# Hybrid decoder step on one core: gate rows ahead of sample factors, projections' second halves in another accumulator ring, old x ahead of output weights

## Chip, cores and metric

The kernel runs on one core of one Trainium2 chip. The metric is the device time of one execution in microseconds; lower is better. The kernel before takes 1245.87 us, the median of three runs (1245.64 to 1247.6).

## The reference, cut to what matters

The program computes one inference step of a two-layer decoder trunk, in float32, for a prompt of 512 positions and 8 single-token samples. Both share the weights, so the kernel treats them as 520 columns (T = 520, TP = 512, TS = 8). The width is 1024, the heads are 4 of 256.

```python
def block(x, c, C0, n0, m0, mbuf0, cbuf0, ...):
    mod = jax.nn.silu(c) @ w_ada + b_ada
    shift, scale, gate = jnp.split(mod[:, None, :], 3, axis=-1)
    h = rmsnorm(x, norm_w) * (1.0 + scale) + shift
    xm, zm, ga, gb, zc, gm, gc = jnp.split(h @ w_in, N_SPLITS, axis=-1)
    xm_c, mbuf = causal_dwconv(xm, mbuf0, mconv_w, mconv_b)
    xm_c = jax.nn.silu(xm_c)
    q = jnp.einsum('bthd,hde->bthe', xc_h, w_q)
    k = jnp.einsum('bthd,hde->bthe', xc_h, w_k) * (HEAD_DIM ** -0.5)
    v = jnp.einsum('bthd,hde->bthe', xm_h, w_v)
    g = (qkv @ w_gate + b_gate).astype(jnp.float32)
    i_pre = jnp.swapaxes(g[..., :N_HEADS], 1, 2)
    logf = jnp.swapaxes(jax.nn.log_sigmoid(g[..., N_HEADS:]), 1, 2)
    hm, C, n, m = mlstm_chunkwise(q, k, v, i_pre, logf, C0, n0, m0)
    ...
    u, cbuf = causal_dwconv(ga * jax.nn.sigmoid(gb), cbuf0, cconv_w, cconv_b)
    ...
    merged = jax.nn.sigmoid(gm) * y_m + jax.nn.sigmoid(gc) * y_c
    x = x + gate * (merged @ w_out)
```

The outputs are x after a last norm, and for prompt and samples the new memories C, n, m and the tails of both convolutions.

## The kernel before, in words

Activations lie with channels on the 128 partitions and positions along the free side: 8 tiles of 128 x 520 for a width of 1024. Every float32 product is made of three in a rounded type: a weight tile is cast (`whi`, on ScalarE, L171) and its remainder taken (`wlo`, on GpSimd, four pieces, L174); activations are split likewise (`hh`, `hl`). `dense` (L178) computes one output tile in two halves of 260 columns; each half is an accumulation of 3 matmuls per input tile, 24 for a width of 1024 and 6 for the per-head projections of q, k and v, and ends with an evacuation by ScalarE or VectorE.

Accumulators come from rings of buffers: tag "d" with three for `dense`, tag "m" with three for nearly all else (gate products `pg` and `pf`, the turned gate rows `pst`, sample values `pvt`, value and key transposes `ptok`, score products `pu` and `pds`, the short convolution's accumulator `ac`), tag "cv" with two for the long convolution. A tile waits until the buffer that it is given has been read by its last reader.

Raw weights come by DMA from SyncE's queue (SP), in order, into two buffers; `whi` and `wlo` have three. So a weight load waits for a `wlo`, and a cast waits until TensorE has finished with the weights of three tiles earlier.

A layer runs so: the norm of x with scale and shift gives `hh` and `hl` (`norm_in`, L435); the first product of the convolution branch; for each head `do_xm` (two tiles of xm, the short convolution, then `xcs`, its split), `do_v` and `do_qk` (both through `proj`, L587); gate products and the scans along the positions (L681 to L728); the convolution branch's next products `gab`; the transposes of the gate rows and of the values; a loop over heads with the scores, and with the samples' memories between; then the remaining products, and at the end the output product, which adds the gated result to the old x (`residual`, L323). In layer 0 the old x is loaded tile by tile into `xo`, one of four buffers of tag "t520" (L1113).

In the gate part (L708 to L728), `st` holds rows that are turned (L735) and copied to `stT` (L737), the per-position factors of the scores. `ur` holds rows for the scores in two parts (L714, L715). `lms`, `mn`, `sx` and `xe` (L716 to L728) are the samples' factors, needed by `sample_factors` after head 0's scores; `sxt` is the tile that holds both `st` and `xe`.

The order on each engine is fixed when the program is built: a scheduler plays through the operations with its own estimates and lists each engine's instructions. `tc.issue_after(i)` tells it that a block may not be listed before instruction i. The engines then run their lists in order.

Of the kernel before, what the change touches and what calls it, by code (L numbers as in the profile page):

```python
# [11 lines left out]
F32 = mybir.dt.float32  # L12
F32R = mybir.dt.float32r
I32 = mybir.dt.int32
AF = mybir.ActivationFunctionType
# [8 lines left out]
TP = 512  # L24
# [49 lines left out]
def build(nc, tc, ctx, ap):  # L74
# [103 lines left out]
    def dense(w, xh, xl, nk, evac, halves=(0, 1)):  # L178
        hi, lo = w
        for c in halves:  # L180
            p = pm("pd", "d")
# [230 lines left out]
    for l in range(L):  # L412
# [22 lines left out]
        def norm_in(k):  # L435
# [8 lines left out]
            else:  # L444
                for c in range(2):
                    v.scalar_tensor_tensor(out=t[:, HALF[c]], in0=x[:, k, HALF[c]], scalar=sa[:, k, 0:1], in1=rb[c],
                                           op0=ALU.mult, op1=ALU.mult)
# [13 lines left out]

        u = None
# [124 lines left out]
        def proj(w, src, dst, h, sc):  # L587
            for m in range(2):
                wm = tuple(a[:, m * 256:(m + 1) * 256] for a in w)
                if sc is None:  # L590
                    dense(wm, src[:, 0], src[:, 1], 2, lambda c, p: s.copy(dst[:, 2 * h + m, c], p))
                else:
                    mm = dense(wm, src[:, 0], src[:, 1], 2,
                               lambda c, p: s.activation(dst[:, 2 * h + m, c], p, AF.Copy, scale=sc))
            return mm if sc is not None else None
# [119 lines left out]
        v.tensor_tensor(out=ur[32:48], in0=gF, in1=ur.bitcast(F32)[0:16], op=ALU.subtract)  # L715
        lms = sml.tile([16, TS], F32, name="lms")  # L716
        mn = sml.tile([16, TS], F32, name="mn")
        v.tensor_tensor(out=lms, in0=lf[:, TP:T], in1=rows[0:16, 1:9], op=ALU.add)
        v.tensor_tensor(out=mn, in0=lms, in1=gi[:, TP:T], op=ALU.max)
        nc.sync.dma_start(ap["o_m_s"][l], mn[0:4])  # L720
        sx = sml.tile([16, 3, TS], F32, name="sx")
        v.tensor_tensor(out=sx[:, 0], in0=lms, in1=mn, op=ALU.subtract)
        v.tensor_tensor(out=sx[:, 1], in0=gi[:, TP:T], in1=mn, op=ALU.subtract)
        v.tensor_scalar(out=sx[:, 2], in0=mn, scalar1=-1.0, scalar2=None, op0=ALU.mult)
        s.activation(sx, sx, AF.Exp)
        for hh_ in range(4):
            v.tensor_scalar(out=xe[0:4, :, hh_, S0:32], in0=sx[0:4], scalar1=ident[0:4, hh_:hh_ + 1],
                            scalar2=None, op0=ALU.mult)  # L728
# [505 lines left out]
```

## Time and profile before

| | |
|---|---|
| Median of three runs | 1245.87 us |
| Profiled execution, its time | 1245.75 us |
| Its span, first to last instruction | 1244.0 us |
| Mean granted TensorE clock | 0.992 |
| TensorE, VectorE, ScalarE, GpSimd busy | 97%, 68%, 44%, 52% |
| Gate part and transposes, layer 0 and 1 | 126 to 155 us, 739 to 767 us |
| Projections, layer 0 and 1 | 58 to 126 us, 666 to 739 us |
| Output product of layer 0, norm of layer 1 | 580 to 626 us, 626 to 651 us |

In the profile PE is TensorE's matmuls, PEld its weight loads, DVE VectorE, ACT ScalarE, POOL GpSimd, and SP the queue that issues DMAs. A row of a timeline starts with the start in us from the span's beginning and the duration in us; then come engine, line, operation, output tile, input tiles, shapes and count, and in brackets the engine's idle time before it with what ended it. A row that begins with a window A:B lists its length, then busy time and count of PE, PEld, DVE, ACT and POOL, then the granted clock, the DMA share and GB/s.

### The profile page before, as it was taken

What the parts mean: (1) busy time and instruction counts of PE and PEld (TensorE: products, weight loads), DVE (VectorE), ACT (ScalarE), POOL (GpSimd) and SP (SyncE); (2) the same over time, 40 slices, a digit from 0 to 9 for tenths busy, and PEclk for the clock granted to TensorE, in tenths of its full rate; (3) what the DMA queues carried; (4) which work ended last, traced back from release to release, by engine and by line L of the source; (5) the groups of instructions that cost most, each with busy time, mean ns of one, the idle gap of its engine ahead of it and who ended that gap; (6) DMA issues with size and microseconds to landing.
All of it is one profiled execution on the core that took longest, in us unless ns stands there. A gap on an engine that the chain in (4) does not pass through costs nothing.

```text
span 1244.0 us, 26981 instructions
## 1 busy us (share of the span) xinstructions
PE 1207.4 (97%) x10856; PEld 1161.5 (93%) x10856; DVE 850.7 (68%) x1719; ACT 550.0 (44%) x991; POOL 648.6 (52%) x869
## 2 busy tenths in 40 slices
PE   6999999999999999999999999999999999999996
PEld 5999898899999999999988988988999999999995
DVE  6874467676998896654258635667789999937424
ACT  4676556543422223532236656556333222335242
POOL 2575444457544444565627553555665544536571
PEclk9999999999999999999999999999999999999998
DMA  9423447742364242243913234575332222224222
GB/s 362 148 89 94 146 149 256 266 173 95 104 219 153 91 148 86 78 170 130 366 67 96 87 109 175 195 263 213 125 103 94 94 88 100 86 85 137 104 86 69
DMA packets 59934, 177.23 MB, mean 142 GB/s; under 512 B 13408, under 2 KB 21664, under 8 KB 55712
## 3 DMA queue, kind: packets, MB, share of 16 engines
q1 hardware_dynamic: 56928, 167.08, 38.8%
q10 hardware_dynamic: 2880, 8.42, 1.8%
q8 instruction: 85, 1.39, 0.5%
q14 instruction: 41, 0.34, 0.1%
HBM read 149.77 MB, written 25.71 MB: 141 GB/s over the span
## 4 chain that ended last, share of the span: by engine, by line
PE 87%; DVE 4%; issue 3%; ACT 3%; DMA 2%; POOL 1%; SPq 0%; DVEq 0%; ACTq 0%; POOLq 0%
PE pd L186 72%; PE pds L889 3%; PE ppv L855 2%; PE pcf L855 2%; DMA wada<-w_ada 1%; PE ada L293 1%; PE ptok L850 1%; ACT whi L171 1%; PE pqc L789 1%; POOL wlo L174 1%; PE pg L688 1%; PE pd L246 1%; DMA raw<-wst 1%; PE pth L946 1%; PE pu L885 0%
## 5 line engine op out<-in xcount | busy, mean ns | idle before, releaser
L174 POOL TENSOR_TENSOR wlo<-raw,whi 128x256 fp32r<-128x256 f32 x680 | 523.8, 803 | 498.9 <-ACT whi L171 490.5
L186 PE MATMUL pd<-hh,whi 128*128 128x260 f32 x1728 | 494.9, 287 | 0.0
L186 PE MATMUL pd<-hl,whi 128*128 128x260 f32 x1728 | 492.2, 285 | 0.0
L186 PE MATMUL pd<-hh,wlo 128*128 128x260 f32 x1728 | 491.8, 285 | 0.0
L171 ACT CAST whi<-raw 128x1024 fp32r<-128x1024 f32 (+1 forms) x174 | 179.4, 1032 | 365.2 <-PE pd L186 329.7
L186 PEld LDWEIGHTS pd<-hh,whi 128*128 128x128 f32 x1728 | 326.8, 189 | 3.6 <-issue 1.8
L186 PEld LDWEIGHTS pd<-hh,wlo 128*128 128x128 f32 x1728 | 326.9, 189 | 1.8 <-issue 1.2
L186 PEld LDWEIGHTS pd<-hl,whi 128*128 128x128 f32 x1728 | 326.5, 189 | 1.8 <-issue 0.6
L535 DVE SCALAR_TENSOR_TENSOR cv<-u,vec,cv 128x509 f32<-128x509 f32 (+6 forms) x448 | 296.8, 729 | 0.0
L804 DVE SCALAR_TENSOR_TENSOR cb<-vb,wsk,cb 128x257 f32<-128x257 f32 x128 | 75.0, 651 | 1.1 <-ACT cb L802 0.4
L186 PE MATMUL pd<-hmh,whi 128*128 128x260 f32 x256 | 72.3, 282 | 0.0
L186 PE MATMUL pd<-hml,whi 128*128 128x260 f32 x256 | 72.3, 282 | 0.0
L186 PE MATMUL pd<-hmh,wlo 128*128 128x260 f32 x256 | 72.3, 282 | 0.0
L186 PE MATMUL pd<-zl,whi 128*128 128x260 f32 x256 | 71.6, 282 | 0.0
L186 PE MATMUL pd<-zh,wlo 128*128 128x260 f32 x256 | 71.6, 282 | 0.0
L186 PE MATMUL pd<-zh,whi 128*128 128x260 f32 x256 | 71.4, 282 | 0.0
L186 PE MATMUL pd<-mh,whi 128*128 128x260 f32 x224 | 63.1, 282 | 0.0
L186 PE MATMUL pd<-mh,wlo 128*128 128x260 f32 x224 | 63.1, 282 | 0.0
L186 PE MATMUL pd<-ml,whi 128*128 128x260 f32 x224 | 63.1, 282 | 0.0
L326 DVE SCALAR_TENSOR_TENSOR xr<-pd,mod,xo 128x260 f32<-128x260 f32 (+1 forms) x32 | 14.8, 482 | 60.7 <-PE pd L186 33.6
L186 PE MATMUL pd<-xcs,whi 128*128 128x260 f32 x256 | 48.5, 289 | 1.0
L186 PEld LDWEIGHTS pd<-hmh,wlo 128*128 128x128 f32 x256 | 48.2, 188 | 0.0
(304 smaller groups left out, 2236.7 us busy)
## 6 DMA issues: line engine op xcount, KB each, us to landing
raw<-wst SPq DMA_DIRECT2D x160, 512.0 KB, 3.7
wada<-w_ada SPq DMA_DIRECT2D x36, 512.0 KB, 9.1
cb<-C SPq DMA_DIRECT2D x16, 1028.0 KB, 7.8
o_C_s<-cb SPq DMA_DIRECT2D x16, 1028.0 KB, 5.7
vb<-vsc SPq DMA_DIRECT2D x16, 514.0 KB, 6.3
wada<-w_ada ACTq DMA_DIRECT2D x12, 512.0 KB, 8.0
raw<-wqkv SPq DMA_DIRECT2D x8, 512.0 KB, 3.6
x<-x SPq DMA_DIRECT2D x4, 520.0 KB
```

The lines of the kernel that those rows point to most:

```text
L171: s.copy(hi, sl)
L174: g.tensor_tensor(out=lo[:, cs], in0=sl[:, cs], in1=hi.bitcast(F32)[:, cs], op=ALU.subtract)
L186: mm = te.matmul(p[:, 0:HT], a[:, ws], b[:, k, HALF[c]], start=(n == 0), stop=(n == 3 * nk - 1))
L246: mm = te.matmul(p[:, 0:HT], a[:, ws], b[:, k, HALF[c]], start=(k == 0 and i == 0), stop=(k == KT - 1 and i == 2))
L293: mm = te.matmul(acc[32 * j:32 * j + 32, 0:128], cT[:, k, :], raw[k // 2][:, k % 2, j * 128:(j + 1) * 128], start=(n == 0), stop=(n == KT ...
L326: v.scalar_tensor_tensor(out=x[:, m, c.start:c.start + n], in0=p[:, 0:n], scalar=mod[:, 16 + m, 0:1], in1=xo[:, c.start:c.start + n], op0= ...
L535: v.scalar_tensor_tensor(out=acc[a][:, sft:TP], in0=u[:, k, 0:TP - sft], scalar=wcol(sft), in1=acc[a][:, sft:TP], op0=ALU.mult, op1=ALU.add)
L688: te.matmul(pgs[n][32 * j:32 * j + 32, 0:HT], vec[:, o:o + 32], (q, kk, vv)[t][:, k, c], start=(r == 0), stop=(r == 5))
L789: te.matmul(p[32 * h:32 * h + 32, 0:V1], zq[:, o:o + 32], cb[:, k, :], start=(j == 0), stop=(j == 1))
L804: v.scalar_tensor_tensor(out=cb[:, 2 * h + j, :], in0=vb[:, h, :], scalar=wsk[:, h, j, b:b + 1], in1=cb[:, 2 * h + j, :], op0=ALU.mult, op ...
L855: te.matmul(p, a, b, start=(first and n == 0), stop=(last and n == 2))
L889: te.matmul(p[:, 0:n], kk[:, 2 * h + j, t0:t0 + 128], q[:, 2 * h + j, t0:TP], start=(j == 0), stop=(j == 1))
```

## The change

Four things change. First, the samples' factors and the second part of `ur` are written as a block that may not be listed ahead of the copy to `stT`. Second, in `proj` the second half of each output tile takes its accumulator from "m" instead of "d". Third, in layer 1, the first operation of `norm_in` goes tile by tile in order. Fourth, both old x tiles of a pair of output tiles are loaded ahead of that pair's weights.

```diff
-    def dense(w, xh, xl, nk, evac, halves=(0, 1)):
+    def dense(w, xh, xl, nk, evac, halves=(0, 1), homes=(("d", 3), ("d", 3))):
         hi, lo = w
         for c in halves:
-            p = pm("pd", "d")
+            p = pm("pd", *homes[c])
...
                 for c in range(2):
-                    v.scalar_tensor_tensor(out=t[:, HALF[c]], in0=x[:, k, HALF[c]], scalar=sa[:, k, 0:1], in1=rb[c],
-                                           op0=ALU.mult, op1=ALU.mult)
+                    with tc.issue_after(norm_in.last.ins) if norm_in.last else nullcontext():
+                        norm_in.last = v.scalar_tensor_tensor(out=t[:, HALF[c]], in0=x[:, k, HALF[c]],
+                                                              scalar=sa[:, k, 0:1], in1=rb[c],
+                                                              op0=ALU.mult, op1=ALU.mult)
...
+        norm_in.last = None
...
-                if sc is None:
-                    dense(wm, src[:, 0], src[:, 1], 2, lambda c, p: s.copy(dst[:, 2 * h + m, c], p))
-                else:
-                    mm = dense(wm, src[:, 0], src[:, 1], 2,
-                               lambda c, p: s.activation(dst[:, 2 * h + m, c], p, AF.Copy, scale=sc))
-            return mm if sc is not None else None
+                mm = dense(wm, src[:, 0], src[:, 1], 2,
+                           lambda c, p: (s.copy(dst[:, 2 * h + m, c], p) if sc is None else
+                                         s.activation(dst[:, 2 * h + m, c], p, AF.Copy, scale=sc)),
+                           homes=(("d", 3), ("m", 3)))
+            return mm
...
-        v.tensor_tensor(out=ur[32:48], in0=gF, in1=ur.bitcast(F32)[0:16], op=ALU.subtract)
-        lms = sml.tile([16, TS], F32, name="lms")
...
+        def sample_gates():
+            lms = sml.tile([16, TS], F32, name="lms")
+            mn = sml.tile([16, TS], F32, name="mn")
+            v.tensor_tensor(out=lms, in0=lf[:, TP:T], in1=rows[0:16, 1:9], op=ALU.add)
+            v.tensor_tensor(out=mn, in0=lms, in1=gi[:, TP:T], op=ALU.max)
+            nc.sync.dma_start(ap["o_m_s"][l], mn[0:4])
+            sx = sml.tile([16, 3, TS], F32, name="sx")
+            v.tensor_tensor(out=sx[:, 0], in0=lms, in1=mn, op=ALU.subtract)
+            v.tensor_tensor(out=sx[:, 1], in0=gi[:, TP:T], in1=mn, op=ALU.subtract)
+            v.tensor_scalar(out=sx[:, 2], in0=mn, scalar1=-1.0, scalar2=None, op0=ALU.mult)
+            s.activation(sx, sx, AF.Exp)
+            for hh_ in range(4):
+                v.tensor_scalar(out=xe[0:4, :, hh_, S0:32], in0=sx[0:4], scalar1=ident[0:4, hh_:hh_ + 1],
+                                scalar2=None, op0=ALU.mult)
...
-        v.tensor_copy(stT, pt.rearrange("p (b r) -> p b r", b=4)[:, :, 0:36])
+        turned = v.tensor_copy(stT, pt.rearrange("p (b r) -> p b r", b=4)[:, :, 0:36])
+        with tc.issue_after(turned.ins):
+            v.tensor_tensor(out=ur[32:48], in0=gF, in1=ur.bitcast(F32)[0:16], op=ALU.subtract)
+            sample_gates()
...
+            xos = [t520("xo") for _ in range(2)]
+            for j in range(2):
+                nc.sync.dma_start(xos[j], x_src[:, m0 + j, :])
             ws = split_w(ap["wst"][l, PR_OUT + m0 // 2], 2)
             for j in range(2):
                 m = m0 + j
-                xo = t520("xo")
-                nc.sync.dma_start(xo, x_src[:, m, :])
-                mm = dense(ws[j], mh, ml, KT, residual(x, xo, mod, m))
+                mm = dense(ws[j], mh, ml, KT, residual(x, xos[j], mod, m))
```

Line numbers of the changed program are 2 to 5 higher than before behind the first edit. In the rows below a line stands first, then the operation, the tile written and the tiles read.

**Place 1, the gate part of layer 0.** VectorE before, up to the copy to `stT` (`us` is a copy for the long convolution of the samples, `upr` its product, made on GpSimd):

```order
L713 TENSOR_TENSOR g_1718<-g_1718 16x512
L722 TENSOR_TENSOR sx<-lms,mn 16x8
L723 TENSOR_TENSOR sx<-g_1718,mn 16x8
L724 TENSOR_SCALAR sx<-mn 16x8
L508 COPY us<-u 128x8
L714 CAST ur<-g_1718 16x512
L727 TENSOR_SCALAR sxt<-sx,ident 4x3x8 x2
L715 TENSOR_TENSOR ur<-g_1718,ur 16x512
L727 TENSOR_SCALAR sxt<-sx,ident 4x3x8 x2
L513 TENSOR_REDUCE u<-upr 128x8
L514 TENSOR_SCALAR u<-u,vec 128x8
L737 COPY stT<-pst 128x144
```

`lms` (L718) and `mn` (L719) stand a few rows further up. VectorE now:

```order
L715 TENSOR_TENSOR g_1718<-g_1718 16x512
L511 COPY us<-u 128x8
L716 CAST ur<-g_1718 16x512
L516 TENSOR_REDUCE u<-upr 128x8
L517 TENSOR_SCALAR u<-u,vec 128x8
L739 COPY stT<-pst 128x144
L741 TENSOR_TENSOR ur<-g_1718,ur 16x512
L720 TENSOR_TENSOR lms<-g_1718,rows 16x8
L755 COPY vtok<-pvt 128x256
L757 COPY qk<-pvt 128x1
L721 TENSOR_TENSOR mn<-lms,g_1718 16x8
L724 TENSOR_TENSOR sx<-lms,mn 16x8
```

The second part of `ur`, `lms`, `mn`, `sx` and the four `sxt` rows moved behind the copy; the `sxt` rows now stand directly ahead of the split of the values, `v1l`. ScalarE at the same place before, from the samples' exponential `sx` to the first score exponential `dd` (`en` is an exponential of the turned rows, `v1h` the values' cast):

```order
L725 ACT_TABLE_LOAD
L725 ACTIVATE sx<-sx 16x24
L553 COPY sg<-pd 128x260
L171 CAST whi<-raw 128x1024
L553 COPY sg<-pd 128x260
L739 ACTIVATE en<-stT 128x16
L579 ACT_TABLE_LOAD
L579 ACTIVATE sg<-sg 128x520
L872 CAST v1h<-ptok 128x2x256 x2
L892 ACT_TABLE_LOAD
L892 ACTIVATE dd<-pu,stT 128x512
```

ScalarE now:

```order
L556 COPY sg<-pd 128x260
L744 ACT_TABLE_LOAD
L744 ACTIVATE en<-stT 128x16
L582 ACT_TABLE_LOAD
L582 ACTIVATE sg<-sg 128x520
L727 ACT_TABLE_LOAD
L727 ACTIVATE sx<-sx 16x24
L877 CAST v1h<-ptok 128x2x256 x2
L897 ACTIVATE dd<-pu,stT 128x512
```

The exponential `sx` moved behind the sigmoid of `sg`, with its table load; the load ahead of `dd` is gone, so the count of loads is the same.

**Place 2, the projections of layer 1.** ScalarE before, at the values of head 0 (`vv`); the buffer numbers tell the halves apart, in the order of the code 8713, 8721, 8729, 8737:

```order
L608 COPY xm_8641<-pd_8644 128x260
L609 CAST xms_8642<-pd_8644 128x260
L171 CAST whi_8818<-raw_8816 128x1024
L608 COPY xm_8641<-pd_8671 128x260
L609 CAST xms_8642<-pd_8671 128x260
L591 COPY vv_8465<-pd_8713 128x260
L616 ACTIVATE ac_8700<-xm_8641,vec_8297 128x512
L591 COPY vv_8465<-pd_8721 128x260
L631 ACTIVATE xc_8459<-acs_8489,vec_8297 128x8 x2
L591 COPY vv_8465<-pd_8729 128x260
```

ScalarE now (8713 and 8729 are first halves, in "d"; 8721 and 8737 second halves, in "m"):

```order
L610 COPY xm_8641<-pd_8644 128x260
L611 CAST xms_8642<-pd_8644 128x260
L171 CAST whi_8818<-raw_8816 128x1024
L610 COPY xm_8641<-pd_8671 128x260
L611 CAST xms_8642<-pd_8671 128x260
L594 COPY vv_8465<-pd_8713 128x260
L618 ACTIVATE ac_8700<-xm_8641,vec_8297 128x512
L594 COPY vv_8465<-pd_8729 128x260
L594 COPY vv_8465<-pd_8721 128x260
```

The cast `whi_8818` stands where it stood, ahead of the two evacuations of 8671. The first half 8729 moved ahead of the second half 8721; TensorE has the same order, and puts all three ahead of the next dense product, 8745, where before all four halves stood ahead of it.

**Place 3, the end of the projections of layer 0.** TensorE before, from the last but one half to the first gate product:

```order
L186 MATMUL pd_1693<-xcs_1638,wlo_1632 128x260
L186 MATMUL pd_1701<-xcs_1638,whi_1631 128x260 x2
L186 MATMUL pd_1701<-xcs_1638,wlo_1632 128x260
L186 MATMUL pd_1701<-xcs_1638,whi_1631 128x260 x2
L186 MATMUL pd_1701<-xcs_1638,wlo_1632 128x260
L688 MATMUL pg_1721<-vv_613,vec_322 32x260 x2
```

TensorE now:

```order
L186 MATMUL pd_1693<-xcs_1638,wlo_1632 128x260
L186 MATMUL pd_1812<-hh_303,whi_1795 128x260
L186 MATMUL pd_1812<-hl_304,whi_1795 128x260
L186 MATMUL pd_1812<-hh_303,wlo_1796 128x260
L186 MATMUL pd_1701<-xcs_1638,whi_1631 128x260 x2
L186 MATMUL pd_1701<-xcs_1638,wlo_1632 128x260
L186 MATMUL pd_1701<-xcs_1638,whi_1631 128x260 x2
L186 MATMUL pd_1701<-xcs_1638,wlo_1632 128x260
L186 MATMUL pd_1812<-hh_303,whi_1795 128x260
L186 MATMUL pd_1812<-hl_304,whi_1795 128x260
L186 MATMUL pd_1812<-hh_303,wlo_1796 128x260
L690 MATMUL pg_1721<-vv_613,vec_322 32x260 x2
```

Six matmuls of the next product, 1812, moved ahead of the gate products; layer 1 has the same. In the whole gate part 117 of them instead of 123 then stand between the second `pf` and `pst`.

Elsewhere: in the norm of layer 1 VectorE does both halves of a tile before the next tile, so the first tile's are the first two of the 8 that stand ahead of the first `hl`, with 2 small ones (`hs`) where 3 stood. TensorE has 36 matmuls of the modulation ahead of the last column sums where it had 48. On SP the two loads of a pair of `xo` stand together, ahead of the weights' loads of the pair after.

More of the change, by code (lines that the diff above doesn't have):

```diff
@@ L714, in build @@
         v.tensor_copy(ur[0:16], gF)
-        v.tensor_tensor(out=ur[32:48], in0=gF, in1=ur.bitcast(F32)[0:16], op=ALU.subtract)
-        lms = sml.tile([16, TS], F32, name="lms")
[L717 to L728, printed above, removed]
+        def sample_gates():
[12 more added lines that the diff above has]
+                                scalar2=None, op0=ALU.mult)
         gab(1, raw=True)
```

## The prediction

> **What bounds the kernel now.** I read the page first, then the chain of waits, then what TensorE itself waits for.
>
> ```profile
> PE 1207.4 (97%) x10856; PEld 1161.5 (93%) x10856; DVE 850.7 (68%) x1719; ACT 550.0 (44%) x991; POOL 648.6 (52%) x869
> PE 87%; DVE 4%; issue 3%; ACT 3%; DMA 2%; POOL 1%; SPq 0%; DVEq 0%; ACTq 0%; POOLq 0%
> 292.06 65.43 PE pd L186 x544
> ```
>
> TensorE (PE) is busy 97% of 1244.0 us. The change removes no matmul, so all it can win is idle TensorE time and time at a lower clock. The third row, a stretch of the chain without a gap, gives the pace: 65.43 / 544 = 0.12 us from one matmul to the next. The waits of TensorE by engine and line say where the idle time is:
>
> ```profile
> PE ptok L850 <- DVE stT L737: 4.6, 2, 2.3
> PE pd L186 <- ACT xms L609: 3.5, 6, 2.7
> PE pd L186 <- ACT kk L594: 1.5, 2, 0.8
> ```
>
> The columns are total us, times, longest. The first row is once per layer: the value transposes (ptok) need an "m" buffer that the turned gate rows (pst) hold until VectorE (DVE) has copied them to stT. The other two lie in the projections. Next the granted clock, in windows (after the idle or busy time of each engine stand PEclk, DMA share and GB/s):
>
> ```profile
> 155.24:158.65 3.41, 3.41 (x17) 3.31 (x16) 1.29 (x2) 3.38 (x5) 0.23 (x1) 0.50 0.97 372
> 670.65:674.06 3.41, 3.40 (x15) 3.40 (x16) 3.41 (x7) 2.99 (x8) 2.88 (x5) 0.50 0.06 9
> 674.06:677.47 3.41, 3.41 (x31) 3.41 (x30) 3.41 (x7) 2.63 (x6) 2.85 (x4) 1.00 0.44 156
> 762.81:766.22 3.41, 1.45 (x38) 1.23 (x36) 3.31 (x14) 1.69 (x4) 2.09 (x3) 1.00 0.35 67
> 11.88:15.29 3.41, 1.86 (x52) 1.05 (x44) 2.88 (x10) 0.00 (x0) 0.00 (x0) 1.00 1.04 401
> PEclk9999999999999999999999999999999999999998
> ```
>
> Behind each wait of 2.3 us or more follows a stretch of 3.41 us at clock 0.50 (the third begins at 766.22, behind the wait in the fourth row). Such a stretch gets 16 matmuls done where a full one gets 31, so it costs 3.41 x (1 - 16/31) = 1.65 us on top of its wait. In the fourth row 1.96 us of 3.41 were idle and the clock fell; in the fifth 1.55 us were idle and it held. I take the limit to lie between the two. The last row, the clock in tenths over 40 slices, shows no other stretch that is long enough to see, but for the tail.
>
> **Part 1, gate rows ahead of sample factors.** VectorE from the end of the scans to the copy:
>
> ```profile
> 147.24 0.62 DVE L718 TENSOR_TENSOR lms<-g,rows 16x8 f32<-16x8 f32 x1
> 147.79 0.67 DVE L711 TENSOR_TENSOR sxt<-g 16x512 f32<-16x512 f32 x1
> 149.38 0.59 DVE L719 TENSOR_TENSOR mn<-lms,g 16x8 f32<-16x8 f32 x1
> 149.89 0.41 DVE L560 TENSOR_TENSOR u<-pd,sg 128x260 f32<-128x260 f32 x1
> 150.83 0.15 DVE L722 TENSOR_TENSOR sx<-lms,mn 16x8 f32<-16x8 f32 x1
> 151.06 0.15 DVE L508 COPY us<-u 128x8 f32<-128x8 f32 x1
> 151.47 0.36 DVE L727 TENSOR_SCALAR sxt<-sx,ident 4x24 f32<-4x24 f32 x2
> 152.90 0.58 DVE L513 TENSOR_REDUCE u<-upr 128x8 f32<-128x248 f32 x1
> 154.02 0.29 DVE L737 COPY stT<-pst 128x144 f32<-128x144 f32 x1
> 157.03 1.29 DVE L873 TENSOR_TENSOR v1l<-ptok,v1h 128x512 fp32r<-128x512 f32 x2 [1.86 <-ACT v1h L872]
> ```
>
> Taken out ahead of the copy, by differences of starts: L718 0.55, L719 0.51, L722 to L724 (150.83 to 151.06) 0.23, and L727, L715, L727 (151.47 to 152.90) 1.43; together 2.72 us. Not all of it comes through: the reduction L513 needs the product that GpSimd makes from the us copy.
>
> ```profile
> 151.29 0.74 POOL L512 TENSOR_TENSOR upr<-us,vec 128x248 f32<-128x248 f32 x1 [1.34 <-DVE us L508]
> ```
>
> The us copy now starts 0.55 + 0.51 + 0.23 = 1.29 earlier, at 149.77; GpSimd is free at 149.95 (151.29 less its idle 1.34), its product ends about 150.75, and L513 starts about 150.8 instead of 150.2. So the copy comes 152.90 - 150.8 = **2.1 us earlier**. Bounds: 2.7, if the product hides, and 1.4, if it takes twice its 0.74.
>
> What is late next? The sample factors' chain, and with it the value copies. ScalarE (ACT) now:
>
> ```profile
> 154.35 0.22 ACT L739 ACTIVATE en<-stT 128x16 f32<-128x16 f32 x1 [1.49 <-DVE stT L737]
> 154.58 1.28 ACT L579 ACT_TABLE_LOAD   x1
> 155.88 0.64 ACT L579 ACTIVATE sg<-sg 128x520 f32<-128x520 f32 x1
> 156.42 1.06 ACT L872 CAST v1h<-ptok 128x512 fp32r<-128x512 f32 x2
> ```
>
> The sample exponential and its table load move between sg and the v1h casts, while the load ahead of L892 goes: as many loads as before, but one is now ahead of v1h. From the end of stT: en 0.22, load 1.28, sg 0.64, load 1.28, sx 0.22 make 3.65; the four L727 (0.15 apart) end at 4.4 and the first v1l (0.65) at 5.1. The score product pds takes the buffer that this v1l frees. TensorE, at full clock, comes there after 4 transposes, pu and 15 + 17 matmuls: 32 x 0.12 and, as an estimate, 0.1 for each of the six small ones = 4.4. So it waits **0.7 us per layer** anew (bounds 0 and 2.0, one more load), too short for the clock. At half clock it came there at 5.4 or later by the same count and would not wait.
>
> **Part 2, projections.** By tile, the idle time before these matmuls is the last number before the arrow, or the last of the row:
>
> ```profile
> L186 PE MATMUL pd<-xms,whi 128*128 128x260 f32 x128 | 26.0, 300 | 5.1 <-ACT xms L609 3.5 <-ACT kk L594 1.5
> L186 PE MATMUL pd<-xcs,whi 128*128 128x260 f32 x256 | 48.5, 289 | 1.0
> 667.99:670.66 2.67, 0.00 (x0) 0.00 (x0) 2.67 (x6) 1.65 (x4) 0.52 (x1) 1.00 0.71 218
> 669.01 1.04 ACT L171 CAST whi<-raw 128x1024 fp32r<-128x1024 f32 x1 [2.46 <-DMA raw<-wqkv]
> ```
>
> Together 6.1 us. Three "d" buffers serve both the projections and the dense products, and a half waits for the evacuation of the one three before. With second halves in "m" the evacuation has some 0.7 us (6 x 0.12) more, against waits of 0.1 to 0.8: I take all of these but 0.2 us as gone. The long one, 2.67, is layer 1's: the evacuations stand on ScalarE behind a weight cast that waits 2.46 us for its DMA. The change leaves that order alone; TensorE gets one more half done first (the order's vv rows: 8729 before 8721), 0.7 us, and 1.95 remain. Gain **6.1 - 1.95 - 0.2 = 3.95 us** (bounds 2.0 and 6.1). The idle 1.95 is as long as in the fourth clock row, so I leave this third stretch at clock 0.50 in the sum.
>
> Six matmuls of the next product now stand ahead of the gate products pg. They are moved, not added, but the VectorE chain of part 1, which ends the stage, starts 6 x 0.12 = 0.72 later: **-1.45 us** for two layers. The wait at ptok becomes 2.3 - 2.1 + 0.7 = 0.9 us, below the 1.55 that left the clock alone. So part 1 gains 2 x 2.1 = 4.2, and two clock stretches, 3.3, less 2 x 0.7 = 1.4 for pds: **+6.1 us**.
>
> The short convolution's accumulators (ac) share "m". I cost that at nothing because the ac rows keep their places on ScalarE and the tightest reader, layer 0's last head, has room:
>
> ```profile
> 109.71 0.40 PE L186 MATMUL pd<-xcs,whi 128*128 128x260 f32 x2
> 117.58 0.70 DVE L643 TENSOR_TENSOR xcs<-xc,xcs 128x520 fp32r<-128x520 f32 x1 [0.95 <-ACT xcs L642]
> ```
>
> The last split xcs ends at 118.28. In the new order TensorE asks for it 78 matmuls after 109.71, at 119.1. The cover is 0.8 us.
>
> **Part 3, order in the next layer's norm.**
>
> ```profile
> 632.68 1.13 PE L201 MATMUL rb<-yi,ident 128*128 128x130 f32 x8 [0.37 <-DVE yi L158]
> 633.40 2.46 DVE L446 SCALAR_TENSOR_TENSOR hx<-xr,sa,rb 128x260 f32<-128x260 f32 x6 [0.87 <-PE rb L201]
> 636.82 0.74 DVE L449 SCALAR_TENSOR_TENSOR hl<-hx,mod,hh 128x512 fp32r<-128x512 f32 x1
> 637.62 0.39 PE L246 MATMUL pd<-hl,whi 128*128 128x260 f32 x1 [0.25 <-DVE hl L449]
> ```
>
> The column sums go ahead of 12 more matmuls of the modulation, so rb loses its 0.37. Then 8 hx (2.46 / 6 = 0.40 each) and 2 small ones (0.08 each) stand before the first hl, where 3 small ones stood: 633.40 - 0.37 + 3.36 = 636.4 against 636.82. TensorE waits for that hl, so **0.4 us** (bounds 0 and 1.5, all four waits between 632 and 638).
>
> **Part 4, old x ahead of the weights.**
>
> ```profile
> DVE xr L326 <- DMA xo<-x: 27.0, 7, 5.6
> 512.62 113.02 PE pd L186 x947
> L174 POOL TENSOR_TENSOR wlo<-raw,whi 128x256 fp32r<-128x256 f32 x680 | 523.8, 803 | 498.9 <-ACT whi L171 490.5
> ```
>
> VectorE waits 27 us for old x, but TensorE runs through 113 us without a gap: three "d" buffers of 24 x 0.12 = 2.9 us each cover it. **Nothing** gained. Lost? On SP's queue the second load of a pair waits for the residual of two products earlier, with weight loads behind it: about 1.0 us after a product ends. Those weights wait for a cast (1.04) and four splits (4 x 0.80) after the same end, 4.2 us. So the new wait is covered by 3.2 us; without that cover each pair would put its excess on TensorE.
>
> **Sum**, against the profiled execution's 1245.75: 3.95 - 1.45 + 6.1 + 0.4 = 9.0, so 1236.75 (span 1235.0). The median of the runs is 0.12 above that execution: **1236.9 us**.
>
> **Rivals.** (a) Half clock stays in all three stretches because it doesn't hang on waits of this length. For it: one execution shows just three; against: each begins within 0.9 us of the end of a wait of 2.3 or more. The 3.3 are lost, the 1.4 saved: 1236.9 + 1.9 = 1238.8. The Trainium skill, page "TensorE: Matmul & The Clock Gate", "HAM oscillation — how this bites in real kernels", warns only of idle gaps above about 3.4 us; by that, waits of 2.3 would cost no clock and 1238.8 would come out. The 0.50 rows here speak against it, and the measurement decides.
>
> (b) The turned copy is no earlier, because the reduction's product or the scans' inputs set it: 6.1 is lost, 1243.0. For it: L513 waits on another engine; against: 1.29 us of small operations stood ahead of its source.
>
> (c) Slower: a second half holds the "m" buffer that ac needs, ScalarE starts ac behind a cast that waits 2.46 us for a DMA, and the split xcs comes late for TensorE. In the built program three ac per layer now lie in a buffer that a projection's half had before. With 2.5 us of lateness less the 0.8 of cover, 1.7 idle and a clock stretch of 1.65, that is 3.35 x 6 = 20: 1257. From 2.3 us of lateness without the clock (1.5 x 6 = 9.0) it eats the gain. Against it: the order's unchanged ac rows.
>
> (d) Better: the remaining 1.95 falls across two clock windows and holds the clock (1.65), and pds finds its buffer free (1.4): 1233.9.
>
> **Chances.** My forecast 0.52, (d) 0.15, (a) 0.14, (b) 0.10, (c) 0.06, anything else 0.03. The range 1232.5 to 1241.5 takes in the forecast with its bounds, (a) and (d), and leaves out 0.19. This kernel's runs tell a difference from none at about 0.2%, 2.5 us. Faster: the forecast, (a), (d) and half of (b), 0.86; same 0.07; slower 0.07.
>
> **What would show it.** Right: ptok's wait near 0.9, clock 1.00 behind it, a wait of some 0.7 at pds for v1l, no wait named kk, near 1.95 left at layer 1's xms, xr no longer named behind xo. Wrong: a wait of over 1.6 at ptok, or new waits of xcs on ScalarE or VectorE, or of pd on weights in the output product.

## The result, and the profile after

The changed kernel takes **1233.22 us** (median of 4 runs, 1231.59 to 1234.1), beside 1245.84 for the kernel before in the same comparison. The ratio is 0.9899, with a 95% interval of 0.9885 to 0.9913. That is 12.6 us faster; the forecast was 9.0 us faster, 1236.9, with a range of 1232.5 to 1241.5. The profiled execution has a span of 1229.9 us where the one before had 1244.0. It is the quickest of the four, so its 14.1 us are a little more than the median shows.

The page of the changed kernel, the line of busy times:

```profile
PE 1198.2 (97%) x10856; PEld 1157.0 (94%) x10856; DVE 853.5 (69%) x1719; ACT 547.9 (45%) x991; POOL 648.9 (53%) x869
```

As many matmuls as before, 9.2 us less of busy TensorE. A busy time that falls although no work was taken out means that the instructions themselves got shorter: some of them ran at half clock before, and, as will be seen, some started late without being counted as idle.

The waits of TensorE in the changed kernel (columns: total us, times, longest):

```profile
PE ptok L855 <- DVE stT L739: 2.7, 2, 1.4
PE ppv L860 <- DVE qc L799: 2.0, 6, 0.3
PE pd L186 <- ACT xms L611: 1.8, 1, 1.8
PE adat L302 <- ACT asb L297: 0.8, 1, 0.8
PE pds L894 <- DVE v1l L878: 0.6, 2, 0.3
PE rb L201 <- DVE yi L158: 0.3, 1, 0.3
PE pd L246 <- DVE hl L451: 0.3, 1, 0.3
```

ptok fell from 4.6 to 2.7, kk is not named any more, and of six waits for xms one is left, the long one of layer 1 with 1.8. pds for v1l is new. One wait for asb of 0.8 stands in the norm in place of shorter ones. All idle times of TensorE over 0.12 us in the trace add up to 24.6 us, where they were 29.1.

In all traces the granted clock changes only at borders that lie whole numbers of 3.41 us apart; call the windows between them the grid of an execution (the last section has more on it). Here are this execution's windows around the first ptok wait and around layer 1's long wait (us, busy time and count of PE, PEld, DVE, ACT and POOL, then the granted clock, DMA share and GB/s):

```profile
148.65:152.06 3.41, 2.44 (x20) 2.45 (x21) 3.28 (x11) 2.67 (x5) 2.51 (x3) 1.00 0.61 189
152.06:155.47 3.41, 3.13 (x22) 2.63 (x21) 2.14 (x8) 2.74 (x5) 0.00 (x0) 1.00 0.36 75
660.66:664.07 3.41, 2.64 (x21) 2.33 (x19) 3.41 (x7) 1.14 (x4) 1.24 (x2) 1.00 0.85 241
664.07:667.49 3.42, 2.34 (x19) 2.35 (x20) 3.42 (x7) 3.42 (x11) 2.87 (x4) 1.00 0.25 80
667.49:670.90 3.41, 3.41 (x31) 3.41 (x30) 3.41 (x6) 2.95 (x6) 1.52 (x4) 1.00 0.42 154
```

The clock is 1.00 behind both. Layer 1's wait of 1.84 us lies across a border, so that one window has 0.77 us idle and the next 1.08. In this execution none of the three half-clock stretches is left, not even the third, which the forecast kept.

Where the time went is best seen in the projections. The two stretches of layer 0 and layer 1, first of the kernel before, then of the changed one:

```profile
41.40:126.40 85.00, 83.22 (x672) 80.93 (x670) 56.49 (x93) 58.92 (x133) 55.37 (x78) 1.00 0.34 102
652.00:738.50 86.50, 82.25 (x650) 79.93 (x648) 57.81 (x93) 58.24 (x131) 54.59 (x77) 0.98 0.30 93
```

```profile
41.80:123.20 81.40, 81.27 (x678) 80.98 (x676) 57.35 (x93) 58.00 (x133) 54.52 (x78) 1.00 0.35 104
646.40:727.20 80.80, 78.96 (x658) 78.51 (x657) 58.15 (x93) 56.89 (x131) 54.46 (x77) 1.00 0.32 97
```

In layer 0 the idle time (length less busy time) fell from 1.78 to 0.13, by 1.65. But the stretch became 3.6 us shorter and holds six matmuls more: 3.6 + 6 x 0.12 = 4.3 us. So **2.7 us were lost before in a place that no row of waits shows**. Layer 1: 86.50 - 80.80 + 8 x 0.12 = 6.7; less one half-clock stretch (1.65) and 0.83 of the long wait, about 4.2, where the short waits add up to 1.6. That is what the forecast didn't have.

### The profile page after: what moved, and what is told of

Same layout as the page of the kernel before. It is cut to its first block, busy times and chain, and to the rows that moved or that the text cites. A ratio compares the mean times of both kernels' runs of the same rounds, so it can differ in the third digit from the quotient of the medians.

```text
span 1229.9 us, 26991 instructions
## 1 busy us (share of the span) xinstructions
PE 1198.2 (97%) x10856; PEld 1157.0 (94%) x10856; DVE 853.5 (69%) x1719; ACT 547.9 (45%) x991; POOL 648.9 (53%) x869
## 4 chain that ended last, share of the span: by engine, by line
PE 87%; DVE 5%; DMA 2%; ACT 2%; POOL 2%; issue 1%; SPq 0%; DVEq 0%; POOLq 0%; ACTq 0%
PE pd L186 72%; PE pds L894 3%; PE ppv L860 2%; PE pcf L860 2%; PE pd L246 2%; DMA wada<-w_ada 2%; DVE cv L538 1%; POOL wlo L174 1%; PE ada L293 1%; PE ptok L855 1%; PE pg L690 1%; PE pqc L794 1%; DMA raw<-wst 1%; DVE ac L620 1%; PE pth L951 1%
## 5 line engine op out<-in xcount | busy, mean ns | idle before, releaser
L186 PEld LDWEIGHTS pd<-hml,whi 128*128 128x128 f32 x256 | 48.2, 188 | 0.0
## 6 DMA issues: line engine op xcount, KB each, us to landing
wada<-w_ada SPq DMA_DIRECT2D x36, 512.0 KB, 10.1
```

What stands on the lines that cost most here:

```text
L186: mm = te.matmul(p[:, 0:HT], a[:, ws], b[:, k, HALF[c]], start=(n == 0), stop=(n == 3 * nk - 1))
```

## Experiments

The experiments ran in three groups, each on one chip together with the kernel before; its medians there were 1246.14 (23 runs), 1246.33 (15) and 1246.63 (15). Ratios are against these. The changed kernel ran again beside the last group only.

### The projections' rings alone

```diff
-    def dense(w, xh, xl, nk, evac, halves=(0, 1)):
+    def dense(w, xh, xl, nk, evac, halves=(0, 1), homes=(("d", 3), ("d", 3))):
-            p = pm("pd", "d")
+            p = pm("pd", *homes[c])
...
+                           homes=(("d", 3), ("m", 3)))
```

> The kernel before with the second halves of the projections in the other ring, and nothing else of the change. By the terms of the forecast: 3.95 us of named idle go, 1.45 come back because six matmuls per layer now stand ahead of the gate products, and the three stretches at half clock stay: 2.5 us gained, 1243.3. By the second theory, which the two traces suggest (a stop of TensorE between two matmuls costs about 0.26 us more from start to start than the idle time that the profile names for it, since the idle is counted from the end of a matmul that lasts 0.28 while the next could have started 0.12 after its start, and the first matmuls behind a stop start 0.22 apart): the sum of starts over 0.12 us apart in the projections falls from 4.6 and, without the long wait and the slow stretch, about 4.5 us to 0.4 each, so 8.3 plus 0.8 of the long wait less 1.45, 7.6 us gained, 1238.2. A half-clock stretch more or less in a run moves either by 1.65. If accumulators of the short convolution hold the buffers (rival c), no gain or a loss.

Measured: 1236.56 us, ratio 0.9921 (0.9907 to 0.9935), 9.6 us faster. The forecast had 2.5. One stop, as a place is called here where TensorE starts a matmul later than its pace, shows why. TensorE of the kernel before, then of this one, at the same place of layer 0 (start, duration, in brackets the idle time):

```profile
59.67 0.28 PE L186 MATMUL pd<-xms,wlo 128*128 128x260 f32 x1
60.13 0.51 PE L186 MATMUL pd<-xms,whi 128*128 128x260 f32 x2 [0.18 <-ACT xms L609]
60.47 0.28 PE L186 MATMUL pd<-xms,wlo 128*128 128x260 f32 x1
60.59 0.40 PE L186 MATMUL pd<-xms,whi 128*128 128x260 f32 x2
```

```profile
59.73 0.28 PE L186 MATMUL pd<-xms,wlo 128*128 128x260 f32 x1
59.85 0.40 PE L186 MATMUL pd<-xms,whi 128*128 128x260 f32 x2
60.09 0.28 PE L186 MATMUL pd<-xms,wlo 128*128 128x260 f32 x1
60.21 0.40 PE L186 MATMUL pd<-xms,whi 128*128 128x260 f32 x2
```

Without a stop a start follows the last start after 0.12 us, though a matmul lasts 0.28: its end overlaps the next two. With the stop, the next start comes 0.46 after the last (59.67 to 60.13), 0.34 more than 0.12; the pair behind it takes 0.34 to the next start (60.13 to 60.47) instead of 0.24, 0.10 more. That is 0.44 us lost, and the row names 0.18. The difference has two parts: 0.28 - 0.12 = 0.16 of the matmul before, which the profile counts as busy, and 0.10 at the start of the pair behind the stop. In layer 0's projections the kernel before has nine stops with some idle time, and in all nine the difference is 0.26 to 0.28; with the rings alone one of the nine is left. **A stop costs its named idle time plus 0.26 us.** Other stops have no idle time at all: a start 0.18 or 0.21 after the last one.

The Trainium skill, page "TensorE: Matmul & The Clock Gate", section "Step-by-step: what each phase is for", says that the end of one matmul overlaps the beginning of the next, so that a lone one costs more than one in a stream. The trace agrees (0.28 against 0.12).

The gain is also 2 us above the 7.6 of the second theory. The windows of this run say where they come from:

```profile
PE ptok L849 <- DVE stT L736: 5.5, 2, 2.7
149.59:153.01 3.42, 1.54 (x13) 1.54 (x14) 2.22 (x9) 1.91 (x5) 2.79 (x4) 1.00 0.79 245
153.01:156.42 3.41, 3.41 (x27) 3.16 (x26) 1.29 (x2) 3.38 (x5) 0.00 (x0) 1.00 0.97 354
665.01:668.42 3.41, 1.49 (x13) 1.37 (x12) 3.41 (x8) 3.02 (x8) 1.89 (x3) 1.00 0.48 148
668.42:671.83 3.41, 3.41 (x18) 3.41 (x18) 3.41 (x7) 1.78 (x6) 2.20 (x4) 0.50 0.26 80
```

ptok's wait became longer here, 2.7 us twice, and yet the clock held behind it. The wait of 148.75 to 151.47 lay across two windows of the grid, with 0.84 idle in the first and 1.88 in the second. The wait at 665.13, shorter (1.92) but within one window, brought a half-clock stretch. So the length of a wait alone doesn't decide; its place on the grid does.

### The gate rows alone

```diff
+        def sample_gates():
...
-        v.tensor_copy(stT, pt.rearrange("p (b r) -> p b r", b=4)[:, :, 0:36])
+        turned = v.tensor_copy(stT, pt.rearrange("p (b r) -> p b r", b=4)[:, :, 0:36])
+        with tc.issue_after(turned.ins):
+            v.tensor_tensor(out=ur[32:48], in0=gF, in1=ur.bitcast(F32)[0:16], op=ALU.subtract)
+            sample_gates()
```

> The kernel before with the turned gate rows copied ahead of the sample factors, and nothing else. By the terms of the forecast 2 x 2.1 of waiting and two stretches at half clock (3.3) go and 1.4 come back at pds: 6.1 gained, 1239.7. By what the trace of the changed kernel shows (the copy comes 1.6 us earlier counted from the gate products, and pds waits 0.3, as a stop about 0.6 us): 3.2 + 3.3 - 1.2 = 5.3, 1240.5, with a wait of about 0.7 at ptok and clock 1.00 behind it. If the half clock doesn't hang on these waits (rival a), 3.3 less: 1243.8, and the page shows clock 0.50 behind ptok again.

Measured: 1241.43 us, ratio 0.9964 (0.9950 to 0.9978), 4.7 us faster. The waits of this kernel:

```profile
PE ptok L853 <- DVE stT L737: 1.9, 2, 0.9
PE pds L892 <- DVE v1l L876: 0.6, 2, 0.3
```

ptok waits 0.94 instead of 2.29: with nothing else changed, the copy comes 1.35 us earlier per layer, where the forecast had 2.1 with a lower bound of 1.4. VectorE and GpSimd of the changed kernel show the reasons:

```profile
142.23 1.69 DVE L711 TENSOR_TENSOR_SCAN g<-g 16x512 f32<-16x512 f32 x1
143.85 1.15 DVE L713 TENSOR_TENSOR sxt<-g 16x512 f32<-16x512 f32 x1
147.99 0.61 DVE L516 TENSOR_REDUCE u<-upr 128x8 f32<-128x248 f32 x1 [0.52 <-POOL upr L515]
148.64 0.72 DVE L517 TENSOR_SCALAR u<-u,vec 128x8 f32<-128x8 f32 x1
149.27 0.29 DVE L739 COPY stT<-pst 128x144 f32<-128x144 f32 x1
147.19 0.77 POOL L515 TENSOR_TENSOR upr<-us,vec 128x248 f32<-128x248 f32 x1 [0.70 <-DVE us L511]
```

From the start of the second scan to the copy it is now 149.27 - 142.23 = 7.04 us; before it was 154.02 - 145.61 = 8.41. The wait for GpSimd's product (0.52) is there as foretold. What the forecast did not have: the first subtraction takes 1.15 where it took 0.67, and L517 0.72 where it took 0.59. Why they became longer isn't shown by any run.

### The norm's order, and old x ahead of the weights, each alone

```diff
+                    with tc.issue_after(norm_in.last.ins) if norm_in.last else nullcontext():
```

```diff
+            xos = [t520("xo") for _ in range(2)]
+            for j in range(2):
+                nc.sync.dma_start(xos[j], x_src[:, m0 + j, :])
             ws = split_w(ap["wst"][l, PR_OUT + m0 // 2], 2)
```

> The kernel before with the order of VectorE in the second layer's norm alone. Forecast: 0.4 us gained, 1245.4; from the trace of the changed kernel, where the norm's stretch ended only 0.1 us earlier: 1245.7. Both are within what the runs can tell from no change; the stretch of 630 to 640 us of the trace decides: one wait at adat or hl of 0.6 or more in place of the four, or four short ones.

> The kernel before with old x loaded ahead of the output weights and nothing else. Forecast: no change, 1245.8; TensorE runs through the output product without a wait, and VectorE no longer waits for xo. If the extra gain of the whole change (12.6 measured, 9.0 forecast) came from here, about 3 us faster, 1242.5.

Measured: the norm 1246.08 (ratio 0.9994, 0.9983 to 1.0005), old x 1246.06 (1.0006, 0.9995 to 1.0017): neither can be told from no change, as forecast for the second, and less than the 0.4 hoped for in the first. In the norm the sum of the waits is what it was, 1.6 us; only the names changed. With the order alone the modulation's transpose waits:

```profile
PE adat L302 <- ACT asb L297: 0.8, 1, 0.8
```

The copy asb stands on ScalarE behind activations that wait for the eight hx, which now run in one go. The order of old x did half of what was said on VectorE, 12.1 us of waiting for xo where there were 27.0, and TensorE noticed nothing. The run of old x alone shows something else, though. Its gate part is that of the kernel before, with the same wait of 2.29 at ptok in either layer:

```profile
149.90:153.31 3.41, 2.54 (x48) 2.14 (x46) 3.35 (x14) 1.69 (x4) 1.42 (x3) 1.00 0.16 45
153.31:156.73 3.42, 2.00 (x17) 2.01 (x18) 1.79 (x7) 2.00 (x3) 2.50 (x4) 1.00 0.80 262
156.73:160.14 3.41, 3.41 (x24) 2.90 (x24) 1.56 (x4) 3.07 (x5) 0.00 (x0) 1.00 1.01 376
760.89:764.30 3.41, 1.11 (x9) 0.91 (x10) 3.31 (x11) 1.91 (x6) 2.76 (x4) 1.00 0.38 102
764.30:767.71 3.41, 3.41 (x18) 3.41 (x17) 1.17 (x3) 3.38 (x5) 0.74 (x2) 0.50 0.92 357
```

In layer 0 the wait lies across a border of the grid, 0.87 us on one side and 1.41 on the other, and the clock holds. In layer 1 all 2.30 lie in one window, and the next runs at 0.50. One kernel, two equal waits, two outcomes.

This also explains most of why the times of one kernel lie up to 6 us apart. Each run lists its mean clock. The 53 runs of the kernel before, sorted by it:

```
mean clock      runs   mean us
0.995            7     1243.8
0.993           13     1244.9
0.992           16     1246.5
0.990, 0.991    16     1247.8
```

(One run at 0.989: 1248.1.) At an equal mean clock of 0.995 the parts can be compared with less of the chance of the grid: rings alone 1235.7 (2 runs), 8.1 faster; gate rows alone 1241.8 (2 runs), 2.0 faster; the whole change 1234.4 (4 runs of two comparisons), 9.4 faster. A step of the rounded clock is about 1.2 us, so these differences are good to some 0.6 us. The whole measured gain of 12.6 is then 9.4 of shorter waits and about 3.2 of clock. The mean clock is no exact count of stretches, though: it takes in the last 8 to 12 us of each span, which run at 0.50, and executions without any stretch before that show 0.995 to 0.997. In the profiled executions the stretches can be counted. With 1.65 us taken off for each, the kernel before, norm alone and old x alone come to 1240.8, 1242.3 and 1241.7 us, the rings alone to 1234.0, the gate rows alone to 1239.8, and the changed kernel, profiled twice, to 1231.6 and 1232.0. That is 7.5, 1.8 and 9.8 us of gain, much the same.

### Filling the wait

Before the first value transposes, matmuls are added whose result nobody reads:

```diff
             p = pm("ptok")
+            if src is vv and h == 0 and a == 0:
+                for _ in range(N_FILL):
+                    te.matmul(p[:, 0:128], ident, ident, start=True, stop=True)
```

> The kernel before with 16 more matmuls per layer (identity times identity, 0.125 us each, 2.0 us) written into the value transposes' own buffer ahead of the first of them: the wait at ptok is filled with work that nobody reads, and is about as long in sum. Theory of the clock: a stretch at clock 0.50 follows when TensorE is idle for about 1.9 us or more within one 3.41-us window of a grid that has another phase in each run, and costs 1.65. Then only the long wait of the second layer's projections can bring one: clocks of 0.995 or 0.996 in every run, where the kernel before has 0.990 to 0.995, and 1242 to 1244 us, some 2.5 faster, though no stall of another engine is shorter. Rival: the stretches hang on something else than TensorE's idle time: clocks as before, 1246.1, or slower by what of the added work doesn't fit into the wait (0 to 1 us).

Measured with 16: 1245.73, ratio 0.9998 (0.9989 to 1.0007). No difference, but mean clocks of 0.993 to 0.996. The expectation had the price of a filler wrong:

```profile
151.44 3.84 PE L849 MATMUL ptok<-ident 128*128 128x128 f32 x32
```

Each is two records, 0.24 us together; 16 of them took 3.84 us, 1.55 more than the wait. Its profile has no half-clock stretch ahead of the end; what the clock gave back, the surplus took. So the run doesn't decide by its time, and it was repeated with half:

> As the filling run before, with half as many idle matmuls: there one took 0.24 us and not 0.125, so that they made 3.84 us per layer, more than the wait of 2.29 they were to fill; 8 make 1.92. Theory of the clock (about 1.9 us idle within one 3.41-us window of the grid brings a stretch at 0.50 that costs 1.65): ptok waits about 0.6, nothing else changes, no stretch is left behind ptok, and the run's mean clock is 0.993 to 0.997; the time falls by one to two stretches, to 1243.5 to 1245, against 1246.2. Rival (the stretches don't hang on TensorE's idle time): clocks of 0.990 to 0.995 and 1246.2 or more.

Measured with 8: **1244.55**, ratio 0.9983 (0.9974 to 0.9993), clocks of 0.993 to 0.995 in its 11 runs where the kernel before had 0.990 to 0.993 in the 15 beside them. TensorE and the windows:

```profile
151.83 2.05 PE L849 MATMUL ptok<-ident 128*128 128x128 f32 x16
155.03 0.66 PE L854 MATMUL ptok<-ident,vv 128*128 128x128 f32 x4 [0.71 <-DVE stT L738]
```

```profile
152.50:155.90 3.40, 2.69 (x24) 2.37 (x22) 2.86 (x9) 1.89 (x4) 2.75 (x5) 1.00 0.62 169
155.90:159.30 3.40, 3.40 (x31) 3.40 (x30) 1.29 (x2) 3.37 (x5) 0.21 (x1) 1.00 0.97 364
```

The profile has one stretch left, at 670.37 behind layer 1's long wait, and none behind ptok. The copy comes no earlier (4.05 us after the gate rows' transposes begin, 4.04 in the kernel before), TensorE gets nothing useful done in the wait, and the kernel is 2 us faster: busy work in place of idle time keeps the clock. So the half clock hangs on TensorE's idle time, and rival (a) of the prediction falls.

### What is left: the last long wait, and the buffer of the turned rows

Layer 1's first value projection, with its weights, behind the next product in place of ahead of it:

```diff
-                if j:
+                if j and not (l == 1 and h == 1):
                     between()
...
                 dense(ws[j], hh, hl, KT, ev)
+                if j and l == 1 and h == 1:
+                    between()
```

> The changed kernel with the value projection of layer 1's first head, and its weight load and cast, behind the second product of the next pair in place of ahead of it, so that these evacuations no longer stand behind a cast that waits for its DMA. Theory: the wait of 1.84 us (2.1 from start to start) goes, and with it the last stretch at half clock, which two of four runs had: 1233.2 - 2.1 - 0.8 = 1230.3, clock 0.996 in all runs. Rival: the weights come as late as before and the wait only moves to the value projection or to the queries: 1233.2, or slower.

Measured: 1232.54 (0.9895, 0.9879 to 0.9911), 0.7 below the changed kernel's 1233.22, which the overlapping intervals cannot tell from no change; one of its five runs has a clock of 0.994. The rival was mostly right: the wait moved and split.

```profile
PE pd L186 <- ACT xms L611: 1.1, 2, 0.9
PE pd L186 <- ACT vv L594: 0.7, 1, 0.7
```

The turned rows in the dense products' ring:

```diff
-        pt = pm("pst")
+        pt = pm("pst", "d")
```

> The changed kernel with the turned gate rows in the dense products' ring in place of the transposes' ring, so that the second value transposes have a buffer without waiting for the copy. Theory (a stop costs its named idle time and 0.26 us): 2 x (1.37 + 0.26) = 3.3 us faster, 1230.0; by the named idle time alone 2.7, 1230.5. The buffer is held 3.4 us, the other two cover 5.8 us of products. Rival: the wait goes to pu or pds, which need the next buffers and the same copies: 1 us or less, 1232.2 to 1233.2.

Measured: 1231.68 (0.9890, 0.9874 to 0.9906), 1.5 below, though the intervals still overlap. The wait at ptok is gone; 0.9 per layer came back at pu, which needs the buffer of the value rows.

```profile
PE pu L890 <- DVE mn L721: 1.9, 2, 0.9
```

On top of it, the sample products in that ring too:

```diff
-            p = pm("pqc")
+            p = pm("pqc", "d")
```

> The kernel of the run ahead of it with the sample products pqc in the dense products' ring too. The six waits of ppv for qc, 0.3 us each, go: by named idle time 2.0 us, with 0.26 for each stop 3.6 us, on top of that run: 1228.0 or 1226.4. Rival: the built order now has all of pqc directly behind the value transposes, where its states are not loaded, or the dense products wait for qc: slower than that run.

Measured: 1269.16, ratio 1.0185 (1.0164 to 1.0206), **slower by 23 us** than the kernel before, and by 37.5 than the run that it stands on. The waits for qc are gone, as meant, but the built order now has them far ahead, and others came that are much longer:

```profile
PE pds L894 <- DVE v1l L878: 14.9, 5, 4.7
PE pds L894 <- ACT dd L897: 4.7, 1, 4.7
```

Against the run that it stands on, TensorE's idle time grew by 20.0 us and its busy time by 14.3 in the profiled executions; four windows at 0.50, at 1.65 each, make some 6.6 of the latter, and the rest was not taken apart. The loss resembles what rival (c) described, in another place: a ring that is eased in one stage changes the order and who holds its buffers in the next. Which of these two costs more is not shown.

Last, the sample factors behind the copies out of the value rows' buffer, then both edits together, and beside them the changed kernel itself once more:

```diff
-            sample_gates()
...
+        copied = v.tensor_copy(qk, pv_[:, 256:257])
+        with tc.issue_after(copied.ins):
+            sample_gates()
```

> The changed kernel with the turned gate rows in the dense products' ring, as in an earlier run, where TensorE's wait moved to pu (0.94 us, for a buffer that the value rows held behind small sample operations on VectorE), and now with the sample factors behind the copies out of that buffer. Theory: 0.6 of those 0.94 go in each layer: 1.2 faster than that run at the same clock, 1230.5. Rival: pu waits for the low part of the gate rows, not for the buffer: 1231.7, no gain.

> The run ahead of it, with the late value projection of layer 1's first pair as well. Alone that edit turned a wait of 1.84 into two of 0.91 and 0.69 and took the last half-clock stretch: 0.5 to 1 us faster than the run ahead of it, 1229.7, with a clock of 0.996 or 0.997. Rival: the two edits share nothing but the gain is lost to the two stops: 1230.5.

> The changed kernel itself once more, on the chip of the runs above. By the stops and the clock it is 9.9 us faster than the kernel before at the same mean clock (8.0 and 1.9 for the two parts alone), and the rest of the measured gain is clock: mean clock of 0.994 to 0.996 in each run against 0.989 to 0.995, 1232 to 1234. By the forecast's terms alone 1236.9.

Measured: 1231.39 (0.9877, 0.9863 to 0.9891), **1230.79** (0.9869, 0.9854 to 0.9885), and 1233.35 for the changed kernel (0.9893, 0.9877 to 0.9908). The repeat confirms the result: 1232.04 and 1232.07 at a mean clock of 0.996, 1234.62 and 1234.92 at 0.995. The best version, with the turned rows in the other ring, the sample factors behind the copies and the late projection, is 2.6 us faster than the changed kernel on the same chip; its four runs (1229.97 to 1231.19) all lie below the other's. Its waits:

```profile
PE pu L893 <- DVE lms L722: 0.9, 2, 0.5
PE pd L186 <- ACT xms L611: 1.0, 2, 0.8
PE pd L186 <- ACT vv L594: 0.8, 1, 0.8
```

pu's 0.94 became 0.47 per layer, a gain somewhat less than the 0.6 expected. In layer 0, with and without that edit, pu starts 0.15 us after the end of qk, the last copy out of the value rows' buffer, which points to the buffer and not to the operations that the rows name (mn, lms). In time the edit alone, 1231.39 against 1231.68 on another chip, cannot be told from none.

## Why the prediction was right in sign and low in size

**Part 2, the projections: the term that was mis-sized.** "Gain 6.1 - 1.95 - 0.2 = 3.95 us" took the named idle time of the rows as the price of the waits. The rings alone gained 8.1 at an equal clock. In the traces the gross gain is 4.3 in layer 0, about 4 in layer 1 and 0.8 of the long wait, 9.1, less 2 x 0.43 at ptok. The missing part is 0.26 us for each stop, in some ten stops per layer. The view for it was there: at the pace of 0.12 us, 85.00 us have room for 708 matmuls, the row of layer 0 counts 672, and the 36 missing ones are 4.3 us. Counting matmuls in a stretch, rather than adding up its idle time, would have given the right size. That ptok would wait longer by six matmuls was right in sign; 0.72 per layer was foretold and 0.43 came (2.29 to 2.72).

The mechanism was right otherwise. No wait is named kk, the short ones for xms are gone but one, the long one of layer 1 is 1.84 where 1.95 was foretold, and no new wait of xcs came from ac sharing the ring: rival (c) did not come about.

**Part 1, the gate rows: right, a little high.** 2.1 us per layer were taken, 1.35 came in the run of that part alone, a hair below the lower bound of 1.4. ptok's wait in the changed kernel is 1.36, not 0.9, and still below what would cost the clock. pds waits 0.28 (with the stop's 0.26, 0.54) where 0.7 was taken. Together 2.0 at an equal clock against 4.2 - 1.4 = 2.8.

**The clock: right in what causes it, wrong in that it always comes.** "Two clock stretches, 3.3" was read from one execution in which two of the three waits happened to lie whole within a window and the third with 1.96 of its 2.30 us. That third stretch began at 766.22, 0.34 ahead of its wait's end at 766.56, so it did not follow the wait but came at a border of the grid. In other executions one or two of the waits leave the clock at 1.00. The clock's share of the gain came out about as large (3.2), by chance in part: the profile of the kernel with old x alone has one stretch for three such waits, that of the norm alone three, and the third, which the sum left in, goes too in about half of the runs, if the mean clocks of 0.996 and 0.995 are read as no stretch and one.

**Part 3**: 0.4 was foretold, nothing came. Two steps failed. That rb "loses its 0.37" is one: 0.30 is left (0.37 with the order alone). From the first hx to the first hl 3.39 us pass, near the 3.36 of the sum and hardly less than the 3.42 of before. The other is "TensorE waits for that hl": the transpose of the modulation waits first, for asb on ScalarE (0.83).

**Part 4**: nothing, as foretold, for the reason given. But xr is still named behind xo, with 12.4 us in place of 27.0, which the prediction's list excluded:

```profile
DVE xr L326 <- DMA xo<-x: 12.4, 3, 5.1
```

**The rivals.** (a) fell with the filled wait, (b) with the gate rows alone (1.35 us earlier), (c) did not occur. (d) gave 1233.9 and is nearest by its number, and half of its mechanism is there (the third stretch holds the clock in some runs; pds does wait, but less). Most of what the forecast missed came from neither.

The sum in the forecast's order, at an equal clock: 2.5 foretold and 8.1 measured for the rings, 2.8 and 2.0 for the gate rows, 0.4 and 0 for the norm, 0 and 0 for old x; 5.7 foretold and 9.4 measured together, to which the clock adds 3.3 and about 3.2. The parts alone sum to 10.1; that 0.7 less comes together is within what these comparisons can tell.

## What to carry to other kernels

Price a wait of a pipelined engine by its starts, not by the idle time that the profile names: here each stop of TensorE cost 0.26 us more than its row, so that a dozen waits of 0.15 us are worth more than one of 2. A half-clock stretch that one profile shows behind a wait is a chance, not a fixed cost; take the mean clock of several runs, and compare edits of a per cent or less at an equal mean clock. And where accumulators move to another ring, read the built order of the whole stage, since the same kind of edit gained 8 us in the projections and lost 37 in the sample products.

## What the runs showed of the hardware

The clock is decided on a grid of 3.41 us that has another phase in each execution. In the kernel before the three stretches begin at 155.24, 670.65 and 766.22, which are 151 and 28 windows apart. Over the profiles of the 14 executions, ahead of each program's last 30 us, every full-clock window of the grid with 1.92 us or more of idle TensorE was followed by one at 0.50, none with 1.64 or less was, and between them it went both ways: 1.78 and 1.88 dropped in two executions, 1.75 and 1.88 held in two others. (A window already at 0.50 can be followed by another with less: in the kernel with the sample products in the other ring, one with 0.64 us idle was.) So the limit is near half of the window, and the idle time as the profile names it doesn't mark it sharply. The Trainium skill, page "TensorE: Matmul & The Clock Gate", section "What's actually happening", has the window as free-running and 3413 ns long, and the trace agrees; its section "HAM oscillation — how this bites in real kernels" warns of idle gaps above about 3.4 us only, and here the runs disagree, since waits of 1.92 to 2.67 us were enough.

The beginning shows the same chance: the full clock was first granted between 11.9 us (the kernel before) and 16.1 us (one of the last runs) after the span's start, depending on the execution, and the loads of the modulation, which wait several times 0.6 us there, can bring a stretch as well. It happened once, in the profile of the best version:

```profile
20.71:24.12 3.41, 1.63 (x45) 0.89 (x41) 3.41 (x7) 0.82 (x2) 3.41 (x4) 1.00 1.03 419
24.12:27.53 3.41, 3.41 (x28) 3.02 (x24) 1.24 (x4) 0.27 (x1) 0.56 (x1) 0.50 1.03 416
```
